# The first stage of a two-layer hybrid block by single k tiles, with its loads and constants in a new order, and each norm's root as one power on GpSimd

## The chip, the cores and the metric

The kernel runs on one core of a Trainium2 chip. The metric is the device time of one execution in microseconds (us); lower is better. Runs of one kernel are compared by their median. Engines are called PE (TensorE's matmuls), PEld (its weight loads), DVE (VectorE), ACT (ScalarE), POOL (GpSimd) and SP (SyncE, which issues the weight loads).

## The reference

Two layers over 256 tokens of width 1024. Each layer norms x, projects it, runs sparse attention and a state-space scan side by side, merges them, and adds a convolved, gated feed-forward part behind a second norm. What the change touches are the norms and the first projection:

```python
def rms_norm(x, w):
    y = xf * lax.rsqrt(jnp.mean(xf * xf, axis=-1, keepdims=True) + NORM_EPS)
    return y * w

for l in range(2):
    h = rms_norm(x, norm_mix_w[l])
    x = x + hybrid_mixer(h, w_in[l], ...)      # proj = h @ w_in, split into q, k, v, qi, ki, wi, z, xbc, dt, gates
    h = rms_norm(x, norm_ffn_w[l])
    x = x + conv_glu_ffn(h, ...)
return rms_norm(x, norm_final_w)
```

In the state-space branch there are also four norms over groups of 512 columns per layer, which makes 13 norms in all: two and four in each of two layers, and the last one.

## The kernel before

Every fp32 weight chunk is loaded by SP into one of five `raw` buffers, rounded by ACT into a high part (`whi`, line L199) and by DVE into the rest (`wlo`, L200), and PE makes each product out of three matmuls: high by high, high by low, low by high. `take()` hands out the next chunk; chunks are prepared ahead as buffers allow, three in `wsp` buffers and, for chunks 2 to 7 of a layer, in tiles that are idle at that time (`ebig`, `ehxh`, `ehxl`, `eths`, `eXt`/`epT`). A `raw` buffer is loaded again when DVE has made its `wlo`.

x lies transposed as 8 k tiles of 128 features by 256 tokens. `Normed.ready(k)` makes the scaled high part `uh` (ACT, L326) and the rest `ul` (DVE, L327) of tile k, its square (ACT, L330 and L333), and adds the squares on POOL (L337, `ssq`). `factor()` sums them over the features with four matmuls of ones (L355) into PSUM, and `rsqrt_col` (L273 to L282) turns the result into 1/root with nine small DVE instructions: `nm`, then a first guess and two rounds of refinement into `ny`. `diagonal` (L289, L290) and two matmuls with ones (L298) spread it to a row.

The first stage of a layer multiplies tokens (stationary) by the columns of `w_in` that stand token by token. c = 0 and 1 are the halves of 616 narrow columns (308 each: index queries and keys, their weights, dt), each by 4 chunks of two k tiles; c = 2 to 4 are 512 columns each (k and v, then q). PE's lines there are L549, L550 and L551. Behind c = 1 start the side lanes: `index_stage` (transposes L440, then the index scores L461, whose matmuls use 64 rows of the array each) and `decay_stage` (`ea` at L509 reads the part of `small` that is loaded late). A side step is issued between the chunks, and a list scheduler with a cost model then fixes each engine's order before the run; engines run their lists in order.

At the start SP loads x's first tile, ACT's queue the other seven in three loads, then SP loads `wi` chunks; POOL's queue loads `small` (norm weights first, 8 KB, then the rest) and the constants `ident`, `tri`, `rope` and `cmask`.

Of the kernel before, what the change touches and what calls it, by code (L numbers as in the profile page):

```python
# [32 lines left out]

RAW_BUFS = 5
SPLIT_BUFS = 3

# [26 lines left out]
def hybrid_kernel(ctx: ExitStack, tc: tile.TileContext, a: dict, out: bass.AP):  # L63
# [104 lines left out]

    def load_some():
        while st["dma"] < len(order) and st["dma"] < st["prep"] + RAW_BUFS:  # L170
# [43 lines left out]
    ones = ones_r.bitcast(F32)  # L214
    warm = const.tile([P, 1], F32, name="warm")
    nc.scalar.activation(warm, ones[:, 0:1], AF.Exp)
# [8 lines left out]
    nc.gpsimd.dma_start(small[:, L * KD:], a["small"][:, L * KD:])  # L225
    ident = const.tile([P, P], F32, name="ident")
    nc.gpsimd.dma_start(ident, a["ident"])
    tri = const.tile([P, P], F32, name="tri")
    nc.gpsimd.dma_start(tri, a["tri"])
    rope = const.tile([P, 2, ROPE_W], F32, name="rope")  # L230
    nc.gpsimd.dma_start(rope, a["rope"])
    cmask = const.tile([P, P], F32, name="cmask")
    nc.gpsimd.dma_start(cmask, a["cmask"])
    neg = const.tile([P, P], F32, name="neg")
    nc.vector.tensor_scalar(neg, cmask, -FILL, FILL, op0=OP.mult, op1=OP.add)

# [8 lines left out]
    o0 = _SMALL["cw"][0]  # L245
    nc.vector.tensor_scalar(half, small[:, o0:o0 + L * 5 * XT], 0.5, None, op0=OP.mult)

# [20 lines left out]
    def rsqrt_col(src, n, scale, eps):  # L268

        m = tmp.tile([P, 8], F32, name="nm", tag="nm", bufs=2)[:, :n]  # L270
        y = tmp.tile([P, 8], F32, name="ny", tag="ny", bufs=3)[:, :n]
        t = tmp.tile([P, 8], F32, name="nt", tag="nt", bufs=2)[:, :n]
# [30 lines left out]
    class Normed:  # L303
# [18 lines left out]
        def ready(self, k):  # L322
            x = xT[:, k, :]
            if self.split:
                w = self.nw[:, k:k + 1]
                nc.scalar.activation(self.hi(k), x, AF.Copy, scale=w)  # L326
                nc.vector.scalar_tensor_tensor(self.lo(k), x, w, self.hi(k).bitcast(F32),  # L327
                                               op0=OP.mult, op1=OP.subtract)
            if k == 0:
                nc.scalar.activation(self.acc, x, AF.Square)  # L330
            else:
                sq = tmp.tile([P, T], F32, name="sq", tag="sq", bufs=2)
                nc.scalar.activation(sq, x, AF.Square)  # L333
                if k == KD - 1:
                    self.sq = sq
                else:
                    nc.gpsimd.tensor_add(self.acc, self.acc, sq)  # L337
            if not self.split:
                nc.scalar.activation(self.xw[:, k, :], x, AF.Copy, scale=self.nw[:, k:k + 1])
# [60 lines left out]
    nrm = Normed(sm("nmw", 0))  # L400
    for k in range(KD):
        nrm.ready(k)
    side("norm", nrm.factor(), 2)

    for l in range(L):
# [132 lines left out]

        for c in range(5):
            n = 308 if c < 2 else 512  # L540
            pss = [pst("acc", [P, n], 4) for _ in range(2)]
            for j in range(4):
                wh, wl = take()
                for kk in range(2):
                    k = 2 * j + kk
                    f, e = k == 0, k == KD - 1
                    for t in range(2):
                        s = slice(t * P, (t + 1) * P)
                        nc.tensor.matmul(pss[t], nrm.hi(k)[:, s], wh[:, kk, :], start=f, stop=False)  # L549
                        nc.tensor.matmul(pss[t], nrm.hi(k)[:, s], wl[:, kk, :], start=False, stop=False)  # L550
                        st["mm"] = nc.tensor.matmul(pss[t], nrm.lo(k)[:, s], wh[:, kk, :], start=False, stop=e)  # L551
            for t in range(2):
                r = nrm.cols[:, t:t + 1]
                if c == 0:
                    nc.scalar.activation(tok[t][:, 0:308], pss[t], AF.Copy, scale=r)
                elif c == 1:
                    nc.scalar.activation(tok[t][:, 308:576], pss[t][:, 0:268], AF.Copy, scale=r)
                    nc.scalar.activation(wd[:, t, :], pss[t][:, 268:308], AF.Copy, scale=r)
                elif c == 2:
# [5 lines left out]
            if c == 1:  # L565
                side("attn", index_stage(), 1)
                side("scan", decay_stage(), 1)
            elif c == 2:
                side("attn", heads_stage(1600, 2, kT), 1)
            elif c > 2:  # L570
                side("attn", heads_stage(576 + (c - 3) * 512, 4, qT[c - 3]), 1)
# [422 lines left out]
```

## Time and profile before

| what | value |
|---|---|
| median of 3 runs | 1090.22 us (1088.49 to 1091.21) |
| profiled execution, its own time | 1091.08 us |
| its span in the trace | 1089.1 us |
| PE busy in the span | 1064.4 us (98%) |
| DVE, ACT, POOL busy | 877.9, 696.2, 66.5 us |
| first matmul starts | 9.21 us into the span |
| last matmul starts / the span ends | about 1081 / 1089.1 us |

The span runs from the first to the last instruction of the trace; the execution's own time is 1.98 us longer. A busy PE is not PE at its peak: matmuls are pipelined, so the distance between starts of two matmuls is their real cost, and the duration shown is longer than that.

### The profile page before, as it was taken

To read this page: it belongs to the slowest core of one execution; us is meant where nothing else is said; L and a number is where in the kernel's file an instruction comes from. 1 tells how busy PE (TensorE), PEld (TensorE's weight loads), DVE (VectorE), ACT (ScalarE), POOL (GpSimd) and SP (SyncE) were. 2 spreads that over 40 slices of the span, in tenths; PEclk is the share of its full clock that TensorE was granted. 3 is DMA by queue.
4 is the path that set the end of the run, shared out by engine and by line. 5 is a ranking of instruction groups with operands and counts; after the bars stand their busy time and mean duration, and the time that the engine had idled before them with its cause. 6 is when DMAs were issued, how large, how long until landed. Compare 5 with 4: busy or idle time off the path is not lost.

```text
span 1089.1 us, 22471 instructions
## 1 busy us (share of the span) xinstructions
PE 1064.4 (98%) x8704; PEld 1026.2 (94%) x8704; DVE 877.9 (81%) x1755; ACT 696.2 (64%) x1285; POOL 66.5 (6%) x74
## 2 busy tenths in 40 slices
PE   6999999999999999998999999999999999999997
PEld 5789989999999999998997999999999999999997
DVE  6898988879877899885668999887887878888643
ACT  5658878647555576665555699865665556666552
POOL 3000000022000200000100000000310020000010
PEclk9999999999999999999999999999999999999999
DMA  7546444555677346666645654555567761666661
GB/s 266 183 148 213 151 147 156 161 169 175 194 233 251 117 122 195 194 199 211 183 134 176 224 155 139 164 172 155 175 190 216 246 216 45 182 187 191 180 182 48
DMA packets 52841, 191.82 MB, mean 176 GB/s; under 512 B 5952, under 2 KB 6240, under 8 KB 51712
## 3 DMA queue, kind: packets, MB, share of 16 engines
q1 hardware_dynamic: 50832, 180.31, 53.8%
q0 software_dynamic: 1472, 9.17, 2.3%
q8 instruction: 68, 1.11, 0.4%
q10 hardware_dynamic: 432, 0.92, 0.2%
q14 instruction: 37, 0.30, 0.1%
HBM read 189.26 MB, written 1.11 MB: 175 GB/s over the span
## 4 chain that ended last, share of the span: by engine, by line
PE 85%; DMA 5%; ACT 4%; DVE 3%; issue 2%; DVEq 0%; ACTq 0%; POOLq 0%
PE acc L370 23%; PE acc L371 23%; PE acc L376 23%; PE acc L550 3%; PE acc L551 2%; PE acc L549 2%; DMA bc<-prd 2%; DMA raw<-in_wu_dram 2%; PE sb L705 1%; DVE wlo L200 1%; ACT whi L199 1%; PE sa L461 1%; DVE ul L327 1%; PE sa L589 1%; PE sa L614 1%
## 5 line engine op out<-in xcount | busy, mean ns | idle before, releaser
L199 ACT CAST whi<-raw 128x1024 fp32r<-128x1024 f32 (+2 forms) x320 | 331.9, 1040 | 225.1 <-PE acc L371 168.7
L200 DVE TENSOR_TENSOR wlo<-raw,whi 128x1024 fp32r<-128x1024 f32 (+2 forms) x320 | 387.0, 1212 | 107.5 <-ACT whi L199 103.1
L370 PE MATMUL acc<-hxh,whi 128*128 128x256 f32 x1456 | 353.3, 282 | 1.0 <-ACT ths L657 0.9
L371 PE MATMUL acc<-hxl,whi 128*128 128x256 f32 x1456 | 351.2, 281 | 0.0
L370 PEld LDWEIGHTS acc<-hxh,whi 128*128 128x128 f32 x1456 | 274.6, 189 | 2.7 <-issue 1.1
L371 PEld LDWEIGHTS acc<-hxl,whi 128*128 128x128 f32 x1456 | 274.7, 189 | 2.2 <-issue 1.9
L376 PE MATMUL acc<-hxh,wlo 128*128 128x256 f32 x1456 | 202.2, 280 | 0.0
L376 PEld LDWEIGHTS acc<-hxh,wlo 128*128 128x128 f32 x1456 | 183.0, 189 | 0.7 <-issue 0.7
L370 PE MATMUL acc<-fH,whi 128*128 128x256 f32 x352 | 84.6, 280 | 2.8 <-DVE xT L833 2.8
L371 PE MATMUL acc<-fL,whi 128*128 128x256 f32 x352 | 84.4, 280 | 0.0
L649 DVE SCALAR_TENSOR_TENSOR cv<-acc,half,cv 128x255 f32<-128x255 f32 (+2 forms) x144 | 67.1, 474 | 3.9 <-ACT cv L647 3.4
L370 PEld LDWEIGHTS acc<-fH,whi 128*128 128x128 f32 x352 | 66.6, 190 | 3.1 <-issue 3.0
L851 DVE SCALAR_TENSOR_TENSOR cv<-acc,small,cv 128x255 f32<-128x255 f32 (+1 forms) x144 | 68.4, 477 | 1.3
L371 PEld LDWEIGHTS acc<-fL,whi 128*128 128x128 f32 x352 | 66.6, 189 | 0.0
L370 PE MATMUL acc<-bH,whi 128*128 128x256 f32 x256 | 62.4, 280 | 0.1
L371 PE MATMUL acc<-bL,whi 128*128 128x256 f32 x256 | 62.3, 282 | 0.0
L337 POOL TENSOR_TENSOR ssq<-ssq,sq 128x256 f32<-128x256 f32 x30 | 27.1, 904 | 516.8 <-ACT sq L333 516.2
L549 PE MATMUL acc<-whi,uh 128*128 128x512 f32 (+1 forms) x112 | 42.0, 392 | 9.2 <-ACT whi L199 9.2
L376 PE MATMUL acc<-fH,wlo 128*128 128x256 f32 x352 | 50.1, 281 | 0.0
L370 PEld LDWEIGHTS acc<-bH,whi 128*128 128x128 f32 x256 | 48.1, 188 | 0.4 <-issue 0.4
L371 PEld LDWEIGHTS acc<-bL,whi 128*128 128x128 f32 x256 | 48.2, 188 | 0.0
L695 ACT ACTIVATE bc<-bc,nP 128x128 f32<-128x128 f32 x128 | 39.9, 390 | 11.6 <-DMA bc<-prd 11.5
(281 smaller groups left out, 1873.0 us busy)
## 6 DMA issues: line engine op xcount, KB each, us to landing
raw<-in_wu_dram SPq DMA_DIRECT2D x88, 512.0 KB, 3.6
raw<-in_wx_dram SPq DMA_DIRECT2D x48, 512.0 KB, 3.6
raw<-in_wd_dram SPq DMA_DIRECT2D x38, 512.0 KB, 3.7
raw<-in_wz_dram SPq DMA_DIRECT2D x32, 512.0 KB, 3.6
raw<-in_wp_dram SPq DMA_DIRECT2D x32, 512.0 KB, 4.4
raw<-in_wq_dram SPq DMA_DIRECT2D x24, 512.0 KB, 4.5
raw<-in_wgs_dram SPq DMA_DIRECT2D x16, 512.0 KB, 3.6
bc<-prd POOLq DMA_DIRECT2D x8, 1024.0 KB, 7.3
```

Of the source, the lines that this page charges most:

```text
L199: nc.scalar.copy(out=hi, in_=r)
L200: nc.vector.tensor_sub(lo, r, hi.bitcast(F32))
L337: nc.gpsimd.tensor_add(self.acc, self.acc, sq)
L370: nc.tensor.matmul(ps, wh[:, j, :], hi(k), start=first and j == 0, stop=False)
L371: nc.tensor.matmul(ps, wh[:, j, :], lo(k), start=False, stop=False)
L376: st["mm"] = nc.tensor.matmul(ps, wl[:, j, :], hi(k), start=False, stop=last and j == len(ks) - 1)
L549: nc.tensor.matmul(pss[t], nrm.hi(k)[:, s], wh[:, kk, :], start=f, stop=False)
L550: nc.tensor.matmul(pss[t], nrm.hi(k)[:, s], wl[:, kk, :], start=False, stop=False)
L551: st["mm"] = nc.tensor.matmul(pss[t], nrm.lo(k)[:, s], wh[:, kk, :], start=False, stop=e)
L649: nc.vector.scalar_tensor_tensor(v[:, j:], ps[:, :T - j], cw(l, 3 - j, i), v[:, j:], op0=OP.mult, op1=OP.add)
L695: nc.scalar.activation(E[:, h, :], E[:, h, :], AF.Relu, bias=nP[:, c, 8 * g + h:8 * g + h + 1])
L851: nc.vector.scalar_tensor_tensor(v[:, j:], uu[:, :T - j], fw(l, 2 - j, i), v[:, j:], op0=OP.mult, op1=OP.add)
```

## The change

- The 616 narrow columns are taken as 8 chunks of one k tile by 616 columns. The two halves of both token halves accumulate at once, in two `acc` and two `sa` tiles of PSUM. A new helper `wide` issues, per k tile, all products high by high, then low by high, then high by low; c = 2 to 4 use it too.
- x is loaded by SP in eight single tiles, each in front of the `wi` chunk of the same k (for the first five). The norm weights go to ACT's queue. The other constants are issued by POOL behind the second addition of squares. Nine matmuls of ones by ones (`WARM`, 512 columns each) stand ahead of everything on PE.
- Tile k's parts are made right before its matmuls, its square one tile later. The first norm's `factor()` starts at the eighth chunk, not the third.
- `rsqrt_col` keeps its first DVE instruction; the other eight become one power (exponent -0.5) on POOL, for all 13 norms.

```diff
+WARM = 9
-        for c in range(2):
-            for j in range(4):
-                add(a["wi"][l, c, j], 2, 308)
+        for k in range(KD):
+            add(a["wi"][l, k], 1, 616)
...
-    nc.gpsimd.dma_start(small[:, :L * KD], a["small"][:, :L * KD])
+    nc.scalar.dma_start(small[:, :L * KD], a["small"][:, :L * KD])
...
+    idle = pst("sb", [P, 4, P], 2)
+    for i in range(WARM):
+        nc.tensor.matmul(idle, ones_r, ones_r[:, None, :].to_broadcast([P, 4, P]), start=True, stop=True)
     with tc.high_priority():
-        nc.sync.dma_start(xT[:, 0:1, :], a["x"][:, 0:1, :])
-    nc.scalar.dma_start(xT[:, 1:2, :], a["x"][:, 1:2, :])
-    nc.scalar.dma_start(xT[:, 2:5, :], a["x"][:, 2:5, :])
-    nc.scalar.dma_start(xT[:, 5:8, :], a["x"][:, 5:8, :])
+        for k in range(KD):
+            nc.sync.dma_start(xT[:, k:k + 1, :], a["x"][:, k:k + 1, :])
+            if k < RAW_BUFS:
+                load_some(k + 1)
...
+    def constants():
+        with tc.issue_after(nrm.add.ins):
+            nc.gpsimd.dma_start(ident, a["ident"])
+            nc.gpsimd.dma_start(small[:, L * KD:], a["small"][:, L * KD:])
+            nc.gpsimd.dma_start(tri, a["tri"])
+            nc.gpsimd.dma_start(rope, a["rope"])
+            nc.gpsimd.dma_start(cmask, a["cmask"])
+        nc.vector.tensor_scalar(neg, cmask, -FILL, FILL, op0=OP.mult, op1=OP.add)
+        nc.vector.tensor_scalar(half, small[:, o0:o0 + L * 5 * XT], 0.5, None, op0=OP.mult)
...
         nc.vector.tensor_scalar(m, src, scale, eps, op0=OP.mult, op1=OP.add)
-        nc.vector.tensor_scalar(y.bitcast(I32), m.bitcast(I32), -0.5, float(0x5f3759df), op0=OP.mult, op1=OP.add)
-
-        nc.vector.tensor_mul(t, y, y)
-        nc.vector.tensor_mul(t, t, m)
-        nc.vector.scalar_tensor_tensor(t, t, -10.0 / 3, t, op0=OP.add, op1=OP.mult)
-        nc.vector.scalar_tensor_tensor(y, t, 5.0, y, op0=OP.add, op1=OP.mult)
-        nc.vector.tensor_mul(t, y, y)
-        nc.vector.scalar_tensor_tensor(t, t, -0.5 * 0.375 ** 3, m, op0=OP.mult, op1=OP.mult)
-        nc.vector.scalar_tensor_tensor(y, t, 1.5 * 0.375, y, op0=OP.add, op1=OP.mult)
+        nc.gpsimd.tensor_tensor(y, m, power[:, :n], op=OP.pow)
...
     nrm = Normed(sm("nmw", 0))
-    for k in range(KD):
-        nrm.ready(k)
-    side("norm", nrm.factor(), 2)
+    side("norm", nrm.factor(), 7)
...
+        def wide(pss, ws, hi, lo, first, last):
+
+            halves = [slice(t * P, (t + 1) * P) for t in range(2)]
+            for t, s in enumerate(halves):
+                for ps, w in zip(pss[t], ws):
+                    nc.tensor.matmul(ps, hi[:, s], w[0], start=first, stop=False)
+            for t, s in enumerate(halves):
+                for ps, w in zip(pss[t], ws):
+                    nc.tensor.matmul(ps, lo[:, s], w[0], start=False, stop=False)
+            for t, s in enumerate(halves):
+                for ps, w in zip(pss[t], ws):
+                    st["mm"] = nc.tensor.matmul(ps, hi[:, s], w[1], start=False, stop=last)
+
+        pss = [[pst("acc", [P, 308], 4), pst("sa", [P, 308], 2)] for _ in range(2)]
+        for k in range(KD):
+            if l == 0:
+                nrm.parts(k)
+                for i in ([k - 1] if k < KD - 1 else [k - 1, k]):
+                    if i >= 0:
+                        nrm.square(i)
+                if k == 3:
+                    constants()
+            wh, wl = take()
+            ws = [(wh[:, 0, o:o + 308], wl[:, 0, o:o + 308]) for o in (0, 308)]
+            wide(pss, ws, nrm.hi(k), nrm.lo(k), k == 0, k == KD - 1)
```

Three places of the engines' orders show what that moves. `DMAHW` and `DMASW` name semaphores of loads issued by SP or ACT and by POOL. First SP's list from the program's start, before:

```order
L221 DMA xT<-in_x_dram 128x256
L174 DMA raw<-in_wi_dram 128x616 x4
L174 DMA raw<-in_wi_dram 128x616 [waits DMAHW0_49]
L174 DMA raw<-in_wi_dram 128x616 [waits DMAHW2_49,DMAHW1_49,DVE_49]
```

and now, up to the seventh weight chunk:

```order
L228 DMA xT<-in_x_dram 128x256
L174 DMA raw<-in_wi_dram 128x616 [waits DMAHW0_49]
L228 DMA xT<-in_x_dram 128x256 [waits DMAHW1_49]
L174 DMA raw<-in_wi_dram 128x616 [waits DMAHW2_49]
L174 DMA raw<-in_wi_dram 128x616 [waits DMAHW3_49,DVE_49]
L228 DMA xT<-in_x_dram 128x256 [waits DMAHW4_49]
L174 DMA raw<-in_wi_dram 128x616 [waits DMAHW5_49,DVE_49]
```

(Ahead of these stand x's tiles 0 to 2 and chunks 0 to 2 in turn, without a wait.) x now shares SP's queue with the weights, and x's tiles 5 to 7 stand behind weight loads that wait for DVE.

Second, ACT's list around `ea`, the first reader of the late part of `small`. Before, it stands in the middle of the first stage:

```order
L326 ACTIVATE uh_103<-xT,small 128x256
L509 ACTIVATE ea<-small 128x32 [waits DMASW1_49]
L199 CAST whi<-raw 128x616 [waits DMAHW4_49]
L333 ACTIVATE sq<-xT 128x256 [waits Pool_49]
```

Now it stands behind the last `wi` chunk (`eXt`), with the last two squares of the first norm and the first wide chunks' casts behind it:

```order
L199 CAST eXt<-raw 128x616 [waits DMAHW0_49]
L339 ACTIVATE sq<-xT 128x256 [waits Pool_49]
L513 ACTIVATE ea<-small 128x32 [waits DMASW1_49]
L339 ACTIVATE sq<-xT 128x256 [waits Pool_49] x2
L199 CAST whi<-raw 128x1024 [waits DMAHW1_49]
```

The wait on `small` moved from early in the stage to its end, and the load that it waits for is issued later.

Third, PE's list in layer 0's wide columns, where the index scores (L461, now L465) stand between the projections' matmuls; the number behind `sa` is the PSUM tile. Before:

```order
L549 MATMUL acc_523<-whi_524,uh1_103 128x512
L461 MATMUL sa_493<-kk4_149,qiT_148 128x128 x2
L461 MATMUL sa_536<-kk4_149,qiT_148 128x128 x2
L550 MATMUL acc_522<-wlo_525,uh1_103 128x512
L551 MATMUL acc_522<-whi_524,ul1_105 128x512
```

and now:

```order
L465 MATMUL sa_499<-kk4_130,qiT_129 128x128 x2
L554 MATMUL acc_529<-wlo_532,uh1_121 128x512
L554 MATMUL acc_530<-wlo_532,uh1_121 128x512
L548 MATMUL acc_529<-whi_531,uh1_121 128x512
L548 MATMUL acc_530<-whi_531,uh1_121 128x512
L551 MATMUL acc_529<-whi_531,ul1_123 128x512
L465 MATMUL sa_500<-kk4_130,qiT_129 128x128 x2
```

In layer 0 there are eight such pairs. Before, two times two pairs stood side by side; now each of the eight stands alone, between other matmuls. In layer 1 both programs keep them in fours.

## Rows read from the trace of the kernel before

**Rows 1.** The page's busy times: us, share of the span, instructions.

```profile
PE 1064.4 (98%) x8704; PEld 1026.2 (94%) x8704; DVE 877.9 (81%) x1755; ACT 696.2 (64%) x1285; POOL 66.5 (6%) x74
```

**Rows 2.** PE's waits, longest first: total us, times, longest.

```profile
PE acc L549 <- ACT whi L199: 9.2, 1, 9.2
```

**Rows 3.** Timeline, 0 to 25 us: start, duration, instruction, idle before it.

```profile
7.05 0.51 ACT L326 ACTIVATE uh<-xT,small 128x256 fp32r<-128x256 f32 x1 [4.37 <-DMA small<-in_small_dram]
...
8.47 0.69 ACT L199 CAST whi<-raw 128x616 fp32r<-128x616 f32 x1
...
9.21 0.88 PE L549 MATMUL acc<-whi,uh 128*128 128x308 f32 x2 [9.21 <-ACT whi L199]
```

**Rows 4.** DMA issues in flight at 1.0 to 1.3 us: KB, us to landing.

```profile
raw<-in_wi_dram SPq DMA_DIRECT2D x1, 308.0 KB, 5.3
...
xT<-in_x_dram SPq DMA_DIRECT2D x1, 128.0 KB, 4.2
small<-in_small_dram POOLq DMA_DIRECT2D x1, 8.0 KB, 5.8
```

**Rows 5.** The same at 1.9 to 2.3 us: the rest of `small`.

```profile
small<-in_small_dram POOLq DMA_DIRECT2D x1, 404.0 KB, 7.6
```

**Rows 6.** Timeline of PE in the first stage, 12 to 29 us.

```profile
12.56 0.46 PE L551 MATMUL acc<-whi,ul 128*128 128x308 f32 x1
...
12.82 0.68 PE L549 MATMUL acc<-whi,uh 128*128 128x308 f32 x2
...
13.33 0.31 PE L550 MATMUL acc<-wlo,uh 128*128 128x308 f32 x1
...
16.63 0.41 PE L550 MATMUL acc<-ebig,uh 128*128 128x308 f32 x1 [1.43 <-DVE ebig L200]
...
19.57 0.31 PE L550 MATMUL acc<-ebig,uh 128*128 128x308 f32 x1
...
20.52 0.39 PE L551 MATMUL acc<-ebig,ul 128*128 128x308 f32 x1
...
22.02 0.31 PE L549 MATMUL acc<-ehxh,uh 128*128 128x308 f32 x1
...
22.16 0.30 PE L550 MATMUL acc<-ehxh,uh 128*128 128x308 f32 x1
...
28.62 0.50 PE L549 MATMUL acc<-whi,uh 128*128 128x512 f32 x1
```

**Rows 7.** PE at the end of layer 0: the longest later wait.

```profile
517.25 0.36 PE L370 MATMUL acc<-fH,whi 128*128 128x256 f32 x1 [2.82 <-DVE xT L833]
```

**Rows 8.** Windows there: from:to, length, busy by engine, PEclk, DMA share, GB/s.

```profile
518.00:520.00 2.00, 2.00 (x14) 2.00 (x13) 2.00 (x4) 1.79 (x6) 1.18 (x2) 0.63 0.98 351
...
522.00:524.00 2.00, 2.00 (x20) 2.00 (x19) 1.30 (x1) 0.32 (x1) 0.22 (x1) 1.00 0.01 4
```

**Rows 9.** Timeline of PE, layer 0's index scores (two array instructions per matmul).

```profile
41.52 0.71 PE L461 MATMUL sa<-kk,qiT 64*128 64x128 f32 x4
...
47.82 0.72 PE L461 MATMUL sa<-kk,qiT 64*128 64x128 f32 x8
```

**Rows 10.** Timeline of DVE, then ACT, at the end: the last norm's root.

```profile
1081.41 0.16 DVE L273 TENSOR_SCALAR nm<-sb 128x2 f32<-128x2 f32 x1 [1.84 <-PE sb L355]
...
1082.98 0.16 DVE L282 SCALAR_TENSOR_TENSOR ny<-nt,ny 128x2 f32<-128x2 f32 x1
...
1083.24 1.27 ACT L908 ACTIVATE y<-acc,ny 128x512 f32<-128x512 f32 x2 [2.76 <-DVE ny L282]
```

**Rows 11.** Timeline: the longest of POOL's early additions.

```profile
11.86 1.34 POOL L337 TENSOR_TENSOR ssq<-ssq,sq 128x256 f32<-128x256 f32 x1 [1.04 <-ACT sq L333]
```

**Rows 12.** Timeline around layer 0's feed-forward norm: its diagonal, and PE's use of it.

```profile
368.44 0.69 ACT L289 ACTIVATE dg<-ident,ny 128x128 fp32r<-128x128 f32 x2 [2.88 <-DVE ny L282]
...
371.71 0.28 PE L298 MATMUL sb<-dg,ones 128*128 128x256 f32 x1
```

**Rows 13.** Windows of 20 us behind the first stage: columns as in the windows above.

```profile
100.00:120.00 20.00, 19.48 (x161) 18.97 (x162) 19.25 (x50) 18.54 (x48) 0.00 (x0) 1.00 0.56 172
```

More of the change, by code (lines that the diff above doesn't have):

```diff
@@ L167, in hybrid_kernel, with load_some @@
     raws, splits = {}, {}
-    def load_some():
-        while st["dma"] < len(order) and st["dma"] < st["prep"] + RAW_BUFS:
+    def load_some(until=None):
+        while st["dma"] < len(order) and st["dma"] < (until or st["prep"] + RAW_BUFS):
             i = order[st["dma"]]
@@ L214, in hybrid_kernel @@
     ones = ones_r.bitcast(F32)
[L215 to L216 removed]
+    power = const.tile([P, 2], F32, name="power")
+    nc.scalar.activation(power, ones[:, 0:2], AF.Exp)
+    nc.vector.memset(power, -0.5)
     small = const.tile([P, SMALL_W], F32, name="small")
[L218 removed]
+    nc.scalar.dma_start(small[:, :L * KD], a["small"][:, :L * KD])
     xT = act.tile([P, KD, T], F32, name="xT")
+    idle = pst("sb", [P, 4, P], 2)
+    for i in range(WARM):
+        nc.tensor.matmul(idle, ones_r, ones_r[:, None, :].to_broadcast([P, 4, P]), start=True, stop=True)
     with tc.high_priority():
[L221 to L225 removed]
+        for k in range(KD):
+            nc.sync.dma_start(xT[:, k:k + 1, :], a["x"][:, k:k + 1, :])
+            if k < RAW_BUFS:
+                load_some(k + 1)
     ident = const.tile([P, P], F32, name="ident")
[L227 removed]
     tri = const.tile([P, P], F32, name="tri")
[L229 removed]
     rope = const.tile([P, 2, ROPE_W], F32, name="rope")
[L231 removed]
     cmask = const.tile([P, P], F32, name="cmask")
[L233 removed]
     neg = const.tile([P, P], F32, name="neg")
[L235 removed]
+    def constants():
[7 more added lines that the diff above has]
+        nc.vector.tensor_scalar(half, small[:, o0:o0 + L * 5 * XT], 0.5, None, op0=OP.mult)
     def sm(name, l=None, n=None):
@@ L245, in hybrid_kernel @@
     o0 = _SMALL["cw"][0]
-    nc.vector.tensor_scalar(half, small[:, o0:o0 + L * 5 * XT], 0.5, None, op0=OP.mult)
     def cw(l, j, i):
@@ L322, in ready, with parts @@
         def ready(self, k):
-            x = xT[:, k, :]
+            self.parts(k)
+            self.square(k)
+        def parts(self, k):
             if self.split:
-                w = self.nw[:, k:k + 1]
+                x, w = xT[:, k, :], self.nw[:, k:k + 1]
                 nc.scalar.activation(self.hi(k), x, AF.Copy, scale=w)
@@ L328, in ready, with square @@
                                                op0=OP.mult, op1=OP.subtract)
+        def square(self, k):
+            x = xT[:, k, :]
             if k == 0:
@@ L336, in ready @@
                 else:
-                    nc.gpsimd.tensor_add(self.acc, self.acc, sq)
+                    self.add = nc.gpsimd.tensor_add(self.acc, self.acc, sq)
             if not self.split:
@@ L537, in decay_stage @@
             nc.gpsimd.dma_start(prd, pr)
-        for c in range(5):
-            n = 308 if c < 2 else 512
-            pss = [pst("acc", [P, n], 4) for _ in range(2)]
+        def wide(pss, ws, hi, lo, first, last):
[21 more added lines that the diff above has]
+            wide(pss, ws, nrm.hi(k), nrm.lo(k), k == 0, k == KD - 1)
+        for t in range(2):
+            r = nrm.cols[:, t:t + 1]
+            nc.scalar.activation(tok[t][:, 308:576], pss[t][1][:, 0:268], AF.Copy, scale=r)
+            nc.scalar.activation(wd[:, t, :], pss[t][1][:, 268:308], AF.Copy, scale=r)
+            nc.scalar.activation(tok[t][:, 0:308], pss[t][0], AF.Copy, scale=r)
+        side("attn", index_stage(), 1)
+        side("scan", decay_stage(), 1)
+        for c in range(2, 5):
+            pss = [pst("acc", [P, 512], 4) for _ in range(2)]
             for j in range(4):
@@ L545, in hybrid_kernel @@
                     k = 2 * j + kk
[L546 to L551, printed above, removed]
+                    wide([[ps] for ps in pss], [(wh[:, kk, :], wl[:, kk, :])], nrm.hi(k), nrm.lo(k),
+                         k == 0, k == KD - 1)
             for t in range(2):
                 r = nrm.cols[:, t:t + 1]
[L554 to L559, printed above, removed]
+                if c == 2:
                     nc.scalar.activation(tok[t][:, 1600:1856], pss[t][:, 0:256], AF.Copy, scale=r)
@@ L564, in hybrid_kernel @@
                     nc.scalar.activation(tok[t][:, o:o + 512], pss[t], AF.Copy, scale=r)
[L565 to L568, printed above, removed]
+            if c == 2:
                 side("attn", heads_stage(1600, 2, kT), 1)
-            elif c > 2:
+            else:
                 side("attn", heads_stage(576 + (c - 3) * 512, 4, qT[c - 3]), 1)
```

3 lines of the change are left out of this document (1 added, 2 removed).

## The prediction

> **What bounds the kernel now.** The page's busy times come first: PE is busy for 98% of the span [rows 1], so time can only come from where PE stands still, runs slowly, or does work that it need not. PE's waits name the places: by far the longest is the one before its first matmul, 9.2 us [rows 2]; the longest later one, in the timeline, is 2.82 us at the end of layer 0 [rows 7]. The timeline of the start says what the first wait is made of: ACT stood until 7.05 us for the norm weights (`small`, on POOL's queue), made two tiles' parts and squares, cast the first chunk at 8.47, and PE started 0.74 us after that cast began, at 9.21 [rows 3]. x's first tile and the first weight chunk had been there earlier: 0.74 + 4.2 = 4.9 us and 1.18 + 5.3 = 6.5 us (SP's issues stand at 0.74 and 1.18) [rows 4].
>
> From 9.21 to the first 512-column matmul at 28.62 [rows 3, 6] are 19.41 us for 96 matmuls and the four of L355. At full clock a 308-column matmul costs 0.14 us from start to start (22.02, 22.16), early on 0.26 (12.56, 12.82) [rows 6]. So 96 x 0.14 = 13.44 us were needed, and L355's group cost 0.81 (20.52 - 19.57 less one step of 0.14) [rows 6]. Lost were 19.41 - 13.44 - 0.81 = 5.16 us: 14 matmuls before 13.33 at the low clock, 14 x 0.12 = 1.7; the wait of 1.43 for DVE's `wlo` [rows 6]; the rest, 2.0, is small waits and the wait for the norm's diagonal just before 28.62.
>
> **The change part by part.**
>
> *The start.* The first matmul now needs x0, `small` and chunk 0, then one square, one high part and one cast. Chunk 0 landed at 6.5 us while three loads of ACT's queue competed with it [rows 4]; these are gone from before it, so I take 6.2, and the matmul 0.74 later: 6.9 us. Bounds: a landing as quick as the 128 KB tile's 4.2 us gives 5.4 and, with the cast behind square and high part, 6.4; `small` as late on ACT's queue as it was on POOL's (5.8 after 0.74, so 6.5 us) gives 7.7 [rows 4]. Gain 2.3 us (1.5 to 2.8).
>
> *The clock.* Nine matmuls of 512 columns run at the low clock from about 1.3 us, when `ones` is ready: scaled from 0.26 for 308 columns [rows 6] they take 3.9 us, to about 5.2, about as long as before's PE ran until its steps shortened (9.21 to 13.33 [rows 3, 6], with half a microsecond of waits). Then PE idles until 6.9. Is the gain kept over 1.7 us of idleness? The rows bound it: after 1.43 us of idleness the steps stayed at 0.14 [rows 6]; after 2.82 us [rows 7] the clock went down to a mean of 0.63 of its 2.4 GHz level, so mostly 1.2 GHz, about a microsecond after work began again, and was back within 4 us [rows 8]. 1.7 is nearer to 1.43. I take all of the 1.7 as won, and keep 0 as the other end. The Trainium skill, "TensorE: Matmul & The Clock Gate" (Part 1), says that an idle array falls back to 1.2 GHz and has to earn 2.4 GHz by sustained work; the trace agrees on both levels [rows 8].
>
> *The waits.* The products that need `wlo` come last in each k tile, so the wait of 1.43 goes. Per k tile PE needs 12 x 0.14 = 1.7 us; ACT a cast of 0.69, a part of 0.51 [rows 3] and a square, which overlap by a tenth each; 436 KB at the 351 GB/s of a full stretch [rows 8] take 1.2; so PE sets the pace. For first fills and for the sums' wait at the end I allow 0.6 us. SP's fifth to seventh x tiles wait behind DVE's first `wlo`s, but PE comes to them at 14 us or later, two or more microseconds after they land by my count.
>
> So the 5.16 us lost shrink to 0.6, and one L298 matmul (0.23) that stood before 28.62 now stands behind; the stage ends earlier by 2.3 + 5.16 - 0.23 - 0.6 = 6.6 us. The wide stage's weights don't hold it: their loads wait for the `wlo` of chunk 3 and later in both programs, and these come earlier with the stage.
>
> *The index scores.* A pair of 128 columns alone takes 0.71 us, two pairs side by side 0.72 [rows 9]. The matmuls of neighbouring pairs use different halves of the array and run together. Before, eight pairs of layer 0 stood in six groups, now in eight. Two joins are lost, each of which hid a pair of 128 columns (0.65 net of its overlap with the next matmul): **+1.3 us**. The Trainium skill, "TensorEngine Tiling (Array Packing)" (The Solution), says the same, that tiles of 64 rows work independently; the rows agree, and it speaks against this order.
>
> *The roots.* Eight small DVE instructions less, 13 times, about 0.2 us each: 20 us of DVE, which is not the bound, so nothing by itself. The one place where the chain is bare is the end: from `nm` at 1081.41 to `y` at 1083.24 are 1.83 us [rows 10]. The new chain is `nm` 0.16, two handovers of about 0.24 together, and the power. The trace shows no power. The bounds are a DVE instruction of the same size, 0.16 [rows 10], and POOL's slowest addition with 128 times as many elements, 1.34 [rows 11]; 0.5 is my value, nearer to the low end as there are two elements per partition. Gain 1.83 - 0.9 = 0.9 us (0.1 to 1.3). Inside the program the norm is covered: in the feed-forward norm the diagonal began at 368.44 and PE came for it at 371.71 [rows 12]; PE's list now comes for it ten matmuls (1.2 us) earlier, but the chain is shorter by as much. The cover is gone when the power takes over 2.8 us.
>
> [...]
>
> *Sum.* 6.6 - 1.3 + 0.9 = 6.2 us off. The profiled execution took 1091.08, so 1084.9 in its terms; it lies 0.86 above the median, 1090.22, so the forecast is **1084.0 us** against that.
>
> **The rivals.**
>
> *All goes well*: no wait in the stage, DVE's relief shortens some later waits. Up to 2.5 us more: 1081.5. For it: DVE is 19.25 of 20 us busy just where PE idles half a microsecond [rows 13].
>
> *The clock is not kept*, or not reached: 1.7 us lost again, 1085.7. For it: the 2.82 us wait [rows 7, 8]; against it: the 1.43 us one [rows 6].
>
> *The constants come late.* ACT now meets `ea` at about 16 us (eight k tiles of some 1.25 us from 6 us on), with two squares and the first wide casts behind it, and PE's sums wait for those squares. POOL issues `small`'s rest behind the third tile's square, at about 10.6 us, and with 7.6 us to landing [rows 5] it arrives at 18.2; ACT then ends the squares at 19 and POOL its addition at about 19.6, just when PE comes. Each microsecond later costs one; 3 more give 1087. The Trainium skill, "SBUF — State Buffer" (SBUF: two separate sides), adds that loads from POOL's queue can starve while DVE works in certain modes; DVE is busy then and was idle before. By that rule this rival would come true, with its 1087; no run here shows it.
>
> *The gain is given back.* DVE has to do the same work in the wide stage and behind it, starting with some 2 us more backlog relative to PE; from 100 to 120 us it and ACT are nearly full [rows 13]. If the next 150 us run at DVE's pace, the 6.6 us vanish: about 1090.5, no change.
>
> *The power is slow*, the one that ends on the other side. What is bare grows with its price p: the end loses p - 1.4, each feed-forward norm p - 2.8, each of the two norms ahead of the projections about p - 3. Against 5.3 us (6.6 - 1.3) this decides at p = 3.7 us; at 6 us the time is about 1102. For it: 13 new instructions of a kind that the trace doesn't show; against it: 256 elements per partition take at most 1.34 [rows 11].
>
> **How the numbers follow.** Forecast 0.57 (1082.8 to 1085.2), all well 0.13, clock 0.11, constants 0.06, given back 0.08, slow power 0.05. What a measurement can tell from no change here is 0.3%, 3.3 us: below 1086.95 is faster, above 1093.5 slower. Faster: 0.57 + 0.13 + 0.11 + half of the constants' = 0.84; same: 0.03 + 0.08 and a little of the slow power = 0.12; slower 0.04. The range 1081 to 1087.5 leaves out the given-back and slow cases and the tails of the first two, under 2 in 10.
>
> **What the profile would show.** First matmul near 6.9 us, steps of 0.14 from there; if the clock failed, steps of 0.26 for the first microseconds. First 512-column matmul near 22.0; ACT's wait at `ea`, if any, ended by `small`. Eight separate index-score groups in layer 0. The power's duration on POOL, and `y` about 0.9 us after `nm` starts. The prediction is wrong if PE stands still behind 22 us where it did not before, or if the power takes over 3 us.

## The result, and the profile after

The changed kernel took **1080.23 us** (median of 20 runs, 1076.42 to 1087.49); the kernel before, run beside it, 1087.54 us (20 runs, 1083.34 to 1094.33; the three shown ahead of the prediction are its first). The ratio is 0.9939, 95% interval 0.9923 to 0.9954: by this ratio 6.6 us less (the two medians lie 7.3 us apart), where the sum of the prediction said 6.2. The forecast of 1084.0 us and its range from 1081.0 are missed by 0.8 us at the low end.

The page of the changed kernel, its busy times (as [rows 1]), and PE's waits, the longest first (as [rows 2]: total, times, longest):

```profile
PE 1062.6 (99%) x8713; PEld 1023.9 (95%) x8713; DVE 862.8 (80%) x1652; ACT 694.0 (64%) x1285; POOL 81.7 (8%) x86
```

```profile
PE acc L376 <- DVE xT L857: 4.4, 5, 1.3
PE sb L361 <- POOL ssq L343: 1.5, 1, 1.5
PE sb L225 <- DVE ones L213: 1.3, 1, 1.3
```

The 9.2 us in front of the first matmul are gone. What is left at the start is 1.3 us for the ones, and there is a new wait of 1.5 us for the norm's sum of squares. The timeline of the first stage shows where it comes from (start, duration, instruction, idle before it; rows of all engines in order of time):

```profile
1.32 4.20 PE L225 MATMUL sb<-ones 128*128 128x512 f32 x9 [1.32 <-DVE ones L213]
...
4.93 0.70 ACT L199 CAST whi<-raw 128x616 fp32r<-128x616 f32 x1
...
5.69 0.41 PE L548 MATMUL acc<-whi,uh 128*128 128x308 f32 x1 [0.18 <-ACT whi L199]
5.94 0.30 PE L548 MATMUL sa<-whi,uh 128*128 128x308 f32 x1
6.08 0.30 PE L548 MATMUL acc<-whi,uh 128*128 128x308 f32 x1
...
16.85 0.71 ACT L199 CAST eXt<-raw 128x616 fp32r<-128x616 f32 x1 [2.89 <-DMA raw<-in_wi_dram]
17.47 0.41 ACT L339 ACTIVATE sq<-xT 128x256 f32<-128x256 f32 x1
...
18.02 1.76 POOL L343 TENSOR_TENSOR ssq<-ssq,sq 128x256 f32<-128x256 f32 x2 [3.51 <-ACT ea L513]
...
19.83 0.38 PE L361 MATMUL sb<-ones,ssq 128*128 128x1 f32 x2 [1.49 <-POOL ssq L343]
...
22.10 0.63 PE L548 MATMUL acc<-whi,uh 128*128 128x512 f32 x2
```

PE's narrow matmuls start at 5.69 us instead of 9.21 [rows 3], after only 0.18 us of idleness, and the distance between starts is 0.14 us (5.94, 6.08) from the second on. ACT's list has the last chunk's cast (`eXt`) ahead of the last three squares; ACT stood 2.89 us for that chunk's load, so the squares, POOL's additions and PE's four matmuls of ones (L361) came late one behind the other. The first 512-column matmul stands at 22.10 us, before at 28.62 [rows 6].

The end, as [rows 10], and all 13 powers on POOL (min, median and max ns):

```profile
1070.83 0.16 DVE L281 TENSOR_SCALAR nm<-sb 128x2 f32<-128x2 f32 x1 [1.84 <-PE sb L361]
1071.06 0.70 POOL L282 TENSOR_TENSOR ny<-nm,power 128x2 f32<-128x2 f32 x1 [8.39 <-DVE nm L281]
1071.80 1.26 ACT L932 ACTIVATE y<-acc,ny 128x512 f32<-128x512 f32 x2 [1.90 <-POOL ny L282]
```

```profile
L282 POOL TENSOR_TENSOR ny<-nm,power x13: 699/869/1674, 23.0 to 1071.1; 128x2 f32<-128x2 f32 x13
```

From `nm` to `y` are 0.97 us, before 1.83.

Where the two profiled executions part shows in the start of the same matmul in both (us, read from PE's timelines; the fourth column is a second profile of the changed kernel, below; the last row is the start of the last two matmuls):

| PE reaches | before | after | after, again |
|---|---|---|---|
| first narrow matmul | 9.21 | 5.69 | 5.32 |
| first 512-column matmul | 28.62 | 22.10 | 21.01 |
| first convolution | 70.95 | 65.95 | 64.87 |
| feed-forward, layer 0 | 361.14 | 354.89 | 352.52 |
| layer 1 | 549.20 | 541.11 | 542.45 |
| feed-forward, layer 1 | 891.04 | 883.19 | 884.24 |
| last two matmuls | 1081.23 | 1070.65 | 1070.85 |

The lead is 6.5 us behind the narrow stage, 5.0 at the first convolution and 10.6 at the end, more than the 7.3 us between the medians. Of the growth, 1.25 us come between the first convolution and the feed-forward of layer 0 (290.19 us before, 288.94 after), 1.84 us in the feed-forward of layer 0 (361.14 to 549.20 is 188.06, 354.89 to 541.11 is 186.22) and 2.73 us in that of layer 1 (190.19 against 187.46). In layer 0 PE's wait at the end of the stage is 1.30 us, before 2.82 [rows 7], and the granted clock stays at 1.00 behind it. The windows of layer 1's feed-forward stage, columns as in [rows 8], before and then after, show no wait in either, but another pace:

```profile
940.00:960.00 20.00, 20.00 (x172) 20.00 (x172) 17.60 (x31) 13.03 (x21) 0.00 (x0) 1.00 0.62 185
```

```profile
940.00:960.00 20.00, 20.00 (x179) 20.00 (x178) 17.89 (x31) 13.04 (x22) 0.00 (x0) 1.00 0.65 196
```

PE is busy all the time at a granted clock of 1.00, and makes 172 matmuls in 20 us or 179.

### The profile page after: what moved, and what is told of

Its sections match the earlier page's. It is cut to its first block, busy times and chain, and to the rows that moved or that the text cites. A ratio compares the mean times of both kernels' runs of the same rounds, so it can differ in the third digit from the quotient of the medians.

```text
span 1078.2 us, 22404 instructions
## 1 busy us (share of the span) xinstructions
PE 1062.6 (99%) x8713; PEld 1023.9 (95%) x8713; DVE 862.8 (80%) x1652; ACT 694.0 (64%) x1285; POOL 81.7 (8%) x86
## 3 DMA queue, kind: packets, MB, share of 16 engines
q8 instruction: 69, 1.13, 0.4%
## 4 chain that ended last, share of the span: by engine, by line
PE 88%; DMA 4%; DVE 3%; issue 2%; ACT 2%; POOL 0%; SPq 0%; POOLq 0%; DVEq 0%; ACTq 0%
PE acc L376 24%; PE acc L377 24%; PE acc L382 24%; PE acc L551 2%; PE acc L554 2%; PE acc L548 2%; DMA raw<-in_wu_dram 2%; PE sb L729 1%; PE sa L613 1%; PE sa L465 1%; DVE wlo L200 1%; PE sa L638 1%; DMA bc<-prd 1%; DVE ul L330 1%; DMA raw<-in_wi_dram 1%
## 5 line engine op out<-in xcount | busy, mean ns | idle before, releaser
L382 PEld LDWEIGHTS acc<-fH,wlo 128*128 128x128 f32 x352 | 44.8, 188 | 0.0
```

The costliest lines, as they stand in the source:

```text
L382: st["mm"] = nc.tensor.matmul(ps, wl[:, j, :], hi(k), start=False, stop=last and j == len(ks) - 1)
```

## The experiments

Each run was set against runs of the kernel before on the same chip, and its ratio and 95% interval are to these. Runs of different sets are compared by their ratios, since the median of the kernel before is 1086.86 to 1088.90 us from set to set. Marks such as "first 512-column matmul" are read from PE's timeline.

**The changed kernel again.** No edit.

> The changed kernel once more, nothing edited. In the two profiled runs the spans lie 10.9 us apart, the medians 6.6 us. Of the 10.9 us, about 3 stand at the end of layer 0, where the kernel before waited 2.82 us and lost the clock and the changed one waited 1.3 us and kept it. Theory: the start is worth what the stage shows (first 512-column matmul near 22.1 us, end chain near 1.0 us) in every run, and the 3 us at the end of layer 0 vary from run to run; then this run's wait there differs from 1.3 us by half a microsecond or more and its span from 1078.2 us by more than 1 us. Rival: the 3 us belong to the change (DVE relieved of the roots); then the wait there is 1.3 us again with the full clock and the median stays 6.6 us below before, the rest being lost somewhere else.

Median 1082.09 us (11 runs), ratio 0.9941 (0.9917 to 0.9965), so 6.4 us off: the gain repeats. The profile has nearly the same span (1078.5 us, 1078.2 in the first), where the theory expected more than 1 us of difference, but it is made otherwise: the stage was 1.1 us quicker, the wait at the end of layer 0 longer, and the feed-forward stage of layer 0 slower, though PE waited nowhere in it:

```profile
511.92 0.36 PE L376 MATMUL acc<-fH,whi 128*128 128x256 f32 x1 [2.11 <-DVE xT L857]
```

```profile
420.00:440.00 20.00, 20.00 (x172) 20.00 (x172) 17.07 (x29) 13.31 (x23) 0.00 (x0) 1.00 0.64 187
...
940.00:960.00 20.00, 20.00 (x179) 20.00 (x179) 17.93 (x29) 13.55 (x23) 0.00 (x0) 1.00 0.67 198
```

The pace of 172 is not the old kernel's: here the same program has it in layer 0 and 179 in layer 1. So the theory that the growth of the lead behind the first convolution varies from run to run holds for the 4.6 us of the two feed-forward stages: layer 0's takes 189.93 us here, longer than before, and layer 1's 186.61. The wait at the end of layer 0 varies too (1.30 and 2.11).

**Without the products of ones.**

```diff
-WARM = 9
+WARM = 0
```

> The nine products of ones are left out (their result is not used). Theory of the prediction: they save 1.7 us, since the first 14 matmuls then run at 0.26 us instead of 0.14; first 512-column matmul at 23.8 us instead of 22.1, total 1.7 us more than the changed kernel. Rival: the stage is held at its end by the sums of squares, for which PE waited 1.49 us (18.34 to 19.83 us); a PE that comes 1.7 us later finds them ready, so the first 512-column matmul stands at 22.3 to 22.5 us and the total moves by at most 0.4 us.

Median 1081.35 us, ratio 0.9932 (0.9906 to 0.9959). The rival is nearer: the 23.8 us of the theory did not come. The timeline shows steps of 0.26 us from 5.59 to 9.34 us, and then no wait for the sums:

```profile
20.02 0.28 PE L361 MATMUL sb<-ones,ssq 128*128 128x1 f32 x2
```

The first 512-column matmul stands at 21.77 us, earlier than the 22.3 to 22.5 of the rival too, and between the 22.10 and 21.01 of the two profiles with the products, in which PE waited 1.49 and 0.51 us for the sums. In this edit the scheduler also joined six of the eight index-score pairs, and the first convolution comes 40.70 us behind that matmul instead of 43.85, so the total says nothing of the products.

**The squares ahead of the last cast.** PE's list is unchanged.

```diff
...
-                sq = tmp.tile([P, T], F32, name="sq", tag="sq", bufs=2)
+                tag, n = (("sq", 2), ("cv", 3), ("ct", 3))[k // 3 if self.first else 0]
+                sq = tmp.tile([P, T], F32, name="sq", tag=tag, bufs=n)
...
```

(`self.first` is true for the first norm alone.)

> The squares of the first norm get buffers of their own (idle ones of other stages), so that the last three stand ahead of the last narrow chunk's cast in ScalarE's list; PE's list is the same row by row. Theory: PE's wait of 1.49 us for the sums comes from these squares queueing behind the cast that waits for the last chunk's load until 16.85 us; the wait goes, first 512-column matmul at 20.6 to 20.9 us, total 1.2 to 1.5 us less than the changed kernel. Rival 1: GpSimd's additions are what is late; the wait stays above 1 us. Rival 2: the stage ends earlier, but the wide stage is then held by its weights (load, cast and lower part), and by 70 us nothing of the 1.5 us is left; total the same.

Median 1079.09 us, ratio 0.9916 (0.9895 to 0.9936). The wait for the sums is gone, as the theory said; so the squares behind the cast were its cause. But PE now stood elsewhere in the stage:

```profile
9.28 0.41 PE L551 MATMUL acc<-ebig,uh 128*128 128x308 f32 x1 [0.31 <-ACT ebig L199]
...
15.69 0.41 PE L554 MATMUL acc<-ehxl,ul 128*128 128x308 f32 x1 [0.54 <-DVE ul L331]
...
19.04 0.28 PE L363 MATMUL sb<-ones,ssq 128*128 128x1 f32 x2
```

The first 512-column matmul stands at 21.21 us, 0.9 earlier than in the first profile of the changed kernel and no earlier than in the second; the theory's 20.6 to 20.9 was not reached. The gain in the total is inside the interval.

**The squares ahead and the index scores joined.**

```diff
-                nrm.parts(k)
-                for i in ([k - 1] if k < KD - 1 else [k - 1, k]):
-                    if i >= 0:
-                        nrm.square(i)
+                with tc.high_priority():
+                    nrm.parts(k)
+                    nrm.square(k)
```

> As the run with the squares ahead, and parts and squares are recorded ahead of the chunk's split; with this the eight index-score pairs of layer 0 stand four by four in PE's list (four groups instead of eight). Theory: each join hides a pair (0.65 us of 128 columns, about 1.1 of 256), so two joins of each give 2 x 0.65 + 2 x 1.05 = 3.4 us on top of the squares' 1.5; total 4 to 5 us less than the changed kernel. Rival: joined pairs take the sum of the single ones (a group of four at 1.4 and 2.2 us), or the wide stage is held by its weights; then the total is that of the squares alone.

Median 1077.48 us, ratio 0.9898 (0.9872 to 0.9923). PE's timeline has four groups where the changed kernel has eight (0.71, 0.71, 0.71, 0.71, 1.13, 1.13, 1.13, 1.13):

```profile
40.79 0.72 PE L468 MATMUL sa<-kk,qiT 64*128 64x128 f32 x8
46.65 0.72 PE L468 MATMUL sa<-kk,qiT 64*128 64x128 f32 x8
52.29 1.13 PE L468 MATMUL sa<-kk,qiT 64*128 64x256 f32 x8
58.13 1.14 PE L468 MATMUL sa<-kk,qiT 64*128 64x256 f32 x8
```

Twice the work in the same time, for both widths. From the first 512-column matmul to the feed-forward stage are 327.74 us, with the squares alone 331.54: 3.8 us for the four joins, against 2 x 0.65 + 2 x 1.05 = 3.4 expected. The median is only 1.6 us lower, and the intervals overlap. In the profiled execution PE waited 3.23 us at the end of layer 0 (1.65 in the run before), and layer 1's feed-forward ran at the slow pace; whether the other executions lost the rest there was not shown.

**The old roots in the changed kernel.**

```diff
-        nc.gpsimd.tensor_tensor(y, m, power[:, :n], op=OP.pow)
+        nc.vector.tensor_scalar(y.bitcast(I32), m.bitcast(I32), -0.5, float(0x5f3759df), op0=OP.mult, op1=OP.add)
...
```

> The changed kernel with the root of each norm as before, nine small instructions on VectorE. In layer 0 one of four groups of index scores joins in PE's list (worth about 0.6 us, to be taken off). Theory of the prediction: the roots count at the end only, where nm to y takes 1.83 us again instead of 0.97 (+0.9 us); the stretch from the first convolution to the feed-forward stage of layer 0 stays at 287.6 to 288.9 us as in the changed kernel's two profiles; total +0.3 us with the join. Rival: VectorE's relief is worth 1 to 2.5 us in that stretch, which took 290.19 us in the kernel before; then it is 290 us again, and the total 2 to 3 us above the changed kernel.

Median 1083.12 us, ratio 0.9948 (0.9924 to 0.9971): by the ratios 0.8 to 1.0 us above the changed kernel, too little for the interval. The end takes 1.82 us again (`nm` 1070.15, `y` 1071.97). The convolution to the feed-forward took 289.52 us, but two single pairs of index scores (63.80 and 65.29 us, 1.05 each) had slid behind the first convolution at 62.88; without them it is 287.4. That speaks for the theory. The run showed something else, the start of its narrow stage:

```profile
6.11 0.62 PE L557 MATMUL acc<-whi,uh 128*128 128x308 f32 x1 [0.58 <-ACT whi L199]
6.53 0.46 PE L557 MATMUL sa<-whi,uh 128*128 128x308 f32 x1
6.79 0.46 PE L557 MATMUL acc<-whi,uh 128*128 128x308 f32 x1
```

Here the nine products of ones (4.21 us) and a gap of 0.58 us left PE at steps of 0.26 us until 10.63, and the 512-column matmul came at 22.71. In the run with squares and pairs a gap of 0.59 us left it at 0.14. The two differ already ahead of the gap, in the last four of the nine products, here and then there:

```profile
3.61 1.91 PE L225 MATMUL sb<-ones 128*128 128x512 f32 x4
```

```profile
3.62 1.37 PE L225 MATMUL sb<-ones 128*128 128x512 f32 x4
```

Here all of them start 0.43 us apart, there the last two follow at 0.31 and 0.23: the clock had risen before the gap.

**The kernel before with the power alone.** The same lines the other way round in the kernel before.

> The kernel before with the roots alone moved to GpSimd; five groups of index scores in layer 0 instead of six. Theory of the prediction: 0.9 us less at the end, about 1 us less for the join, the stretch from the first convolution to the feed-forward stage at 290 us as before: 1.9 us below before. Rival: VectorE's relief shows in that stretch, 288 us instead of 290.19, and at the end of layer 0, where the wait of 2.82 us shrinks to 1.3 us: 4 to 5 us below before.

Median 1083.69 us, ratio 0.9964 (0.9942 to 0.9986): 3.9 us below before, between the two; the interval (1.5 to 6.3 us) holds both. In its profile the narrow stage ends 0.9 us earlier (27.70: PE no longer waits for the diagonal), the end takes 0.97 us (`nm` 1074.29, `y` 1075.26), and from there to the feed-forward it is 328.58 us, before 332.52. Of these 3.9 us the joins account for about 1.4: one pair of 128 and two of 256 columns are hidden now (0.65 + 2 x 1.05), two of 128 before (2 x 0.65). From the first convolution to the feed-forward it is 288.40 us instead of 290.19, which speaks for VectorE's relief; the wait at the end of layer 0 is 2.80 us as before, which speaks against it. With the run above: the relief is worth somewhere from nothing to 2 us, and stays open.

**Five powers.**

```diff
         nc.gpsimd.tensor_tensor(y, m, power[:, :n], op=OP.pow)
+        for i in range(4):
+            nc.gpsimd.tensor_tensor(y, y, ones[:, :n], op=OP.pow)
```

> The changed kernel with four more powers, of exponent 1, behind each root: a root then takes five times 0.87 us, 4.35 us, the price at which the prediction's rival of the slow power would decide. One of four groups of index scores in layer 0 joins (-0.6 us). By the prediction's covers: +3.5 us at the end, 4.35 - 2.8 = 1.5 us at each of the two feed-forward norms, 4.35 - 3 = 1.3 us at each norm ahead of the projections, in all +9 us, 1089 us. Rival: inside the program the cover is longer than 4.35 us, and only the end pays: +3 us, 1083 to 1084 us.

Median 1088.64 us, ratio 1.0008 (0.9988 to 1.0027): by the ratios about 7.3 us above the changed kernel, nearer to the 9 of the covers than to the 3 of the end alone. The waits of PE (columns as above):

```profile
PE acc L378 <- DVE xT L859: 5.0, 3, 2.9
PE sb L300 <- ACT dg L291: 2.4, 3, 0.8
PE acc L378 <- DVE cu L893: 1.6, 2, 0.8
PE acc L378 <- DVE ths L843: 1.4, 2, 0.9
```

At the end the five powers took 3.77 us (0.70, and 2.99 for the four added). The end pays 3.1 us; each feed-forward norm 0.6 us (0.80 at `cu` instead of 0.21), less than the 1.5 expected; the two norms ahead of the projections, expected to pay 1.3 each, pay nothing; and three gated norms (those over 512 columns in the state-space branch), which the prediction had not listed, pay 2.4 us at L300. Before these three the five powers took 4.5 to 8.9 us. Five powers bring the time back to that of the kernel before.

**x on ScalarE's queue.**

```diff
-            nc.sync.dma_start(xT[:, k:k + 1, :], a["x"][:, k:k + 1, :])
+            if k == 0:
+                nc.sync.dma_start(xT[:, k:k + 1, :], a["x"][:, k:k + 1, :])
+            elif k in (1, 2, 5):
+                n = {1: 2, 2: 5, 5: 8}[k]
+                nc.scalar.dma_start(xT[:, k:n, :], a["x"][:, k:n, :])
```

> The changed kernel with seven of the eight tiles of x in three loads on ScalarE's queue, as before, instead of one by one between the chunks on SyncE's queue. Theory: the prediction put the first matmul at 6.9 us because it kept chunk 0's landing near the 6.2 us that it had beside such loads; it came at 5.3 to 5.7 us because x's other tiles no longer compete with chunk 0; with them back it is at 6.4 us or later. Rival: those loads cost chunk 0 nothing, and the first matmul stays at 5.3 to 5.9 us.

One run, 1083.47 us. ACT's first cast says when chunk 0 was there:

```profile
6.58 0.70 ACT L199 CAST whi<-raw 128x616 fp32r<-128x616 f32 x1 [2.94 <-DMA raw<-in_wi_dram]
```

6.58 us, against 4.93 in the changed kernel: the theory holds in this one run, x's other tiles cost chunk 0 at least 1.6 us. PE itself started at 11.02, since `small` was issued behind x (at 2.21 us) and the high parts stood late in ACT's list (10.47); that is another order, not the price of the queue.

**The last narrow chunk of layer 1 earlier**, on top of squares and pairs. PE's list is unchanged.

```diff
-             6: (13, "ths", "ths"), 7: (10, "Xt", "pT")}
+             6: (13, "ths", "ths"), 7: (13, "Xt", "pT")}
```

> The kernel with the squares ahead and the index scores joined, and one number more: the last narrow chunk of layer 1 is taken up 13 chunks ahead of the layer's first instead of 10, so its cast stands three chunks earlier in ScalarE's list; TensorE's list is the same row by row. Theory: the wait at the end of layer 0 (1.3 to 3.4 us in every profile, 3.23 us in this kernel's) comes from that cast: ScalarE stood 5.49 us for the chunk's load and the casts, lower parts and residual queued behind it; with three other casts ahead the wait falls below 1 us, and with it the low clock behind it: 2 to 4 us less, about 1074 us. Rival: the loads there set the pace whatever their order, another chunk is late instead, and the wait stays at 1.3 us or more; the total is the same as without it, 1077.5 us.

Median **1074.2 us** (1071.08 to 1077.74), ratio 0.9871 (0.9838 to 0.9904): by the ratio 14.0 us below the kernel before, and the lowest of all. Below squares and pairs alone it lies 2.9 us by the ratios, with intervals that still overlap; the profiles show it in the feed-forward stage of layer 0, 185.04 us instead of 189.44. Without the edit ACT's timeline reads

```profile
500.58 0.71 ACT L199 CAST eXt<-raw 128x616 fp32r<-128x616 f32 x1 [5.49 <-DMA raw<-in_wi_dram]
501.20 2.72 ACT L199 CAST whi<-raw 128x1024 fp32r<-128x1024 f32 x3
```

and with it

```profile
492.26 0.71 ACT L199 CAST eXt<-raw 128x616 fp32r<-128x616 f32 x1 [0.50 <-DMA raw<-in_wi_dram]
492.87 1.05 ACT L199 CAST whi<-raw 128x1024 fp32r<-128x1024 f32 x1
```

The three casts that stood behind `eXt` were what DVE and then PE waited for; PE's wait at the end of layer 0, present in all the profiles above, is not in its list of waits any more, and its clock does not fall there. The edit moves the chunk's load ahead together with its cast; the two were not tested apart.

**All early chunks of layer 1 earlier.**

```diff
-EARLY_MIX = {2: (21, "big0", "big0"), 3: (16, "big1", "big1"), 4: (16, "hxh", "hxh"), 5: (14, "hxl", "hxl"),
-             6: (13, "ths", "ths"), 7: (10, "Xt", "pT")}
+EARLY_MIX = {2: (23, "big0", "big0"), 3: (20, "big1", "big1"), 4: (19, "hxh", "hxh"), 5: (17, "hxl", "hxl"),
+             6: (16, "ths", "ths"), 7: (14, "Xt", "pT")}
```

> As the run with the last narrow chunk earlier, and the other five early chunks of layer 1 are moved two to four chunks earlier too. Theory: each of them stands in ScalarE's list at a place where its load has landed, so the wait at the end of layer 0 goes, as in the other run, and no new one comes: 1073 to 1075 us. Rival: the loads of the last weights of layer 0 are pushed behind them, and the wait only moves to these: 1077 us or more.

Median 1078.65 us, ratio 0.9912 (0.9877 to 0.9947). The rival: the wait moved 22 us ahead, to a weight of the down projection.

```profile
482.86 0.39 PE L378 MATMUL acc<-fH,whi 128*128 128x256 f32 x1 [2.34 <-ACT whi L199]
```

**Without the products of ones where the sums are not waited for.** The kernel with squares and pairs, `WARM = 0`.

> The kernel with the squares ahead and the index scores joined, without the nine products of ones. There TensorE no longer waits for the sums of squares. Theory: what hid the low clock in the changed kernel was that wait; here the first 512-column matmul comes 1.2 to 1.7 us later than the 20.60 us with the products, at 21.8 us or more. Rival: the chunks' loads set the pace of the stage (the DMA engines were busy for 88% of the first 20 us), so it comes at 20.6 to 21.2 us without the products too.

One run, 1075.07 us. The first 512-column matmul came at 21.95 us:

```profile
21.95 0.62 PE L551 MATMUL acc<-whi,uh 128*128 128x512 f32 x2
```

With the products it came at 20.60, 20.45 and 20.88 in three profiles of the same stage; the first of them, squares and pairs:

```profile
20.60 0.39 PE L551 MATMUL acc<-whi,uh 128*128 128x512 f32 x1
```

So the theory, from one run without them: where the sums do not hold the stage, the products are worth 1.1 to 1.5 us. The steps of 0.26 us, the low clock, lasted from 5.28 to 10.06 us.

## Why the prediction was off, step by step

**The number.** The step that failed is the last one: "it lies 0.86 above the median, 1090.22, so the forecast is 1084.0 us against that". The sum was close (6.2 forecast, 6.6 measured by the ratio, interval 5.0 to 8.4), but the level to which it was added was the median of three runs, and that of 20 is 2.7 us lower; the other three sets, of 11 to 29 runs, have medians of 1086.86 to 1088.90. Of the 3.8 us by which 1084.0 missed the 1080.23, 2.7 are this level and 1.1 the change (7.3 us between the medians instead of 6.2). From 1087.54 the same sum gives 1081.3, and the range, moved by as much, is 1078.3 to 1084.8, which holds the measured time. The range was built from the terms alone; single runs of the kernel before spread over 11 us, where the prediction allowed 3.3 for what a measurement can tell from no change, and the level of three of them was taken as exact. A part of that spread shows in the profiles: each layer's feed-forward stage runs at one of two paces, some 4 us apart per layer (next but one section), and the profiled execution of before had the slow one in layer 1. That the paces make the spread of the unprofiled runs as well was not shown.

**The start** was mis-sized: 5.69 us instead of 6.9. Chunk 0 was put at 6.2 us because it had landed at 6.5 beside three other loads [rows 4]; without them it was cast at 4.93, and the run with x on ScalarE's queue brought the late landing back. `small` on ACT's queue did not hold it.

**The waits** were mis-sized the other way. From 5.69 to 22.10 are 16.41 us; 14.25 are needed (13.44 + 0.81), so 2.2 were lost where 0.6 were allowed, 1.49 of them at the sums. The prediction had named the place (the squares behind ACT's list, POOL's addition, PE's sums) in its rival of the late constants, but put it down to `ea` and `small`; it was the cast of the last chunk that held the squares, as the run with the squares ahead showed. The rest of `small`, issued at 9.77 us, landed 6.5 us later, ahead of `ea` at 17.79, with DVE busy for 6.41 of these 6.5 us (before it took 7.6 [rows 5]), so the starving that this rival named did not show. The errors of the start and of the waits offset, which is luck: the first 512-column matmul was forecast for 22.0 and came at 22.10, and in the second profile at 21.01, where PE waited 0.51 us for the sums.

**The clock.** "I take all of the 1.7 as won" came true in the profile (0.14 us from the second step), but it was not worth 1.7 us: without the products the stage ended 0.3 us earlier than in one profile with them and 0.8 later than in the other, since PE then meets the sums when they are ready. Where the sums do not hold the stage the products gave 1.1 to 1.5 us. And they do not always work: of nine profiles with them, one (x on ScalarE's queue) left PE idle for 5.5 us behind them; in the other eight the short steps began at once five times, at 7.0 and 7.3 us in two (five powers, all chunks earlier), and at 10.6 in one (old roots).

**The index scores** are right: eight single groups, and from the first 512-column matmul to the first convolution 43.85 us instead of 42.33, 1.5 against 1.3 forecast.

**The roots** are right at the end (0.86 against 0.9 forecast), with a power of 0.70 us there, not 0.5, and two handovers of 0.11 together, not 0.24. Elsewhere it took up to 1.67 us, under the cover of 2.8, as forecast; with five powers (3.77 us and more) the covers break, at the gated norms too, which the list of covers lacked. The 1.34 us taken for POOL's slowest addition is the longest of the early ones [rows 11]; the same line takes up to 1.80 us later in that trace. Whether VectorE's relief, put at nothing, is worth up to 2 us between the first convolution and the feed-forward stays open. The Trainium skill, "GPSIMD Engine Reference" (3. Performance versus the Vector engine), gives about 156 ns of dispatch for an instruction of DVE, and for GpSimd two software dispatch hops without a figure. So the 156 ns is no price for the power; the rows show 699 to 1674 ns for one of 128x2.

**The end of layer 0** was not forecast to change and varied by itself: 2.82 us before, 1.30 and 2.11 in two profiles of the changed kernel. It comes from a cast that ACT meets before its load has landed, as the run with the last narrow chunk earlier showed, and the kernel before has it too: its ACT stands 5.29 us for `eXt` there, the changed one's 4.73.

## What to carry to other kernels

Add a forecast to a level that enough runs have fixed, and give the range the spread of that level besides the bounds of the terms. A saving at the start of a stage counts only if nothing at its end is late by itself: here most of what the warm clock saved went into a wait on a sum that was late anyway, and it earned its microsecond only when that was cured. A list order that was made with estimated landing times can put one cast in front of three others that are ready; look at what an engine that executes in order stands for, and move that one load, not all of its kind.

## What the hardware showed unexpectedly

- Two paces of PE at the same granted clock of 1.00, with no wait: the 256-column matmuls of a feed-forward stage follow each other at about 0.113 us (179 in 20 us) or 0.118 us (172 to 173) for a whole feed-forward stage, in either layer, in different runs of one program. In layer 1 that stage takes 190.2 to 191.5 us in the four profiles at the slow pace and 186.2 to 187.5 in the nine others. What sets it was not found.
- The same nine products of ones (3.67 to 4.21 us), followed by gaps of 0.58 and 0.59 us, left PE once at steps of 0.26 us (the 1.2 GHz level) and once at 0.14 us (2.4 GHz); in the second case the products themselves had gone over from 0.43 us apart to 0.23. The gap does not decide: with none or 0.1 us the short steps began at once in two profiles and 1.7 us late in two. The granted clock in the windows read 1.00 in the stretch of 0.26 us steps too, so at the start the distance of the starts has to be read, not that column.
- At the end of layer 0 the granted clock fell to 0.50 behind a wait of 2.29 us (without the products) and stayed at 1.00 behind waits of 2.80 and 2.87 us (the power alone, five powers): the length of the wait alone does not tell.
- A power of 128x2 on GpSimd took 0.70 us at best and 1.67 at worst among the 13 of the changed kernel's profile.
